# Running inverse roots of the key norms moved from SBUF into spare PSUM columns in a DeltaNet mixer

## The chip, the core and the metric

The kernel runs on one core of a Trainium2 chip. A core has five engines, each with its own instruction queue that is worked off in order: TensorE (PE in the profile; its weight loads are shown apart as PEld), VectorE (DVE), ScalarE (ACT), GpSimd (POOL) and SyncE (SP, which here only starts transfers). They share the memory SBUF; PE writes its products into PSUM, which DVE and ACT read and write too. Engines wait for each other by semaphores. The metric is the device time of one execution, in microseconds (us); durations of single instructions are also given in us unless ns is written.

## What is computed

Two layers of a diffusion trunk on 512 latent and 256 context tokens of width 1024. Layer 0 mixes tokens by a bidirectional gated DeltaNet, layer 1 by retention; each is followed by a SwiGLU block. The change touches layer 0's mixer, and in one helper every inverse root. What matters of the reference:

```python
def l2norm(t):
    tf = t.astype(jnp.float32)
    return tf * lax.rsqrt(jnp.sum(tf * tf, axis=-1, keepdims=True) + EPS)

def gdn_mixer(...):
    p = t @ w_in
    qkv = jax.nn.silu(short_conv(p[..., :GDN_QKV], conv_w))
    q = l2norm(to_heads(qkv[..., :QK_A], H_A)) * DK_A ** -0.5
    k = l2norm(to_heads(qkv[..., QK_A:2 * QK_A], H_A))
    ...
    # chunked gated delta rule over k, q, v, forward and backward; then
    # o * rsqrt(mean(o * o) + EPS) * g * silu(gate), and a projection
```

There are 8 heads of width 128. The kernel does not scale k itself: it keeps k unnormalised and puts the inverse root r of each token's squared norm, and its square, into the factors that multiply k elsewhere.

## The kernel before

All large products are exact to about fp32: each operand is split into a high and a low part and three matmuls are summed (`mm3`, L129 is the line that issues them). The heads of the DeltaNet go through a pipeline written out by hand. While PE runs the projections of head i+2 (generator `gdn_s1`, products into the PSUM tiles `psg`, of which there are 2), it also runs, interleaved in a fixed order, the triangular inverse of head i+1 (`gdn_merge`) and the output of head i (`gdn_out`). PE's instructions of this part keep the order in which the program writes them; the instructions of DVE, ACT and POOL are put in order by a scheduler ahead of time, from the program's text and an estimate of durations. At run time every engine then works off its list in order, so an instruction that waits holds back all that stand behind it on its engine.

The small tiles of this stage are `psx`: 6 PSUM tiles of 512 fp32 columns, used in rotation.

For every head, at a fixed place among the projection matmuls, `ktr` runs (heads are counted from 0):

- 6 PE transposes of the key chunks `kq` (L137), three into each of two `psx` tiles, columns 0 to 383;
- for each of these halves an ACT square into `sq` (L884), a DVE sum over it into three columns of the SBUF tile `ks` (L885), and an ACT copy of the transposed keys into `kt` (L886);
- one DVE chain on six columns: add EPS (L887), `rsqrt` (L169 and L171 give a first guess by integer arithmetic; three Newton rounds of L174, L175, L176), the norm s*r (L889), r*r (L891), and three products that give `knb`, `kbeta`, `kbd` (L894).

Around it stand these pieces, whose names the prediction uses:

- `gdn_decay`: POOL forms masks `gm` (L957, two buffers of two), PE multiplies them with `sl` into `psx`, ACT takes the exponent into `E` (L963), and POOL masks it (L964). These POOL instructions read SBUF only.
- `gdn_out` of an earlier head: ACT squares `so` (L1060), DVE sums `os` (L1061), a DVE `rsqrt` of the same 11 steps on its own tiles, then six ACT copies of `oa` scaled by that root (L1065).
- `gdn_merge`: PE products of `ysb` with `invt`, then DVE `COPY_PREDICATED` into `inva` (L1185) and a DVE transpose into `invt` (L1188), then PE products of `invt` with `U`.
- `lin`: ACT copies a finished projection out of `psg` into `pb` (L839); ACT and DVE then form the short convolution `cb` (L846, L848). `pb` also frees the `psg` tile for PE.

Of the kernel before, what the change touches and what calls it, by code (L numbers as in the profile page):

```python
# [10 lines left out]
F32 = mybir.dt.float32  # L11
# [5 lines left out]
ALU = mybir.AluOpType  # L17
AX = mybir.AxisListType
# [9 lines left out]
EPS = 1e-6  # L28
# [26 lines left out]
class Trunk:  # L55
# [80 lines left out]
    def tr(self, out, in_, ident):  # L136
        ins = self.nc.tensor.transpose(out, in_, ident)  # L137
        if self.strict:
            self.tc.keep_in_program_order(ins)
# [22 lines left out]
        self.gemm(ps, [tuple(cut(t, k) for t in w) for k in range(KT)], [tuple(t[:, a:b] for t in hk) for hk in h[st]])  # L162
        return ps

    def rsqrt(self, s, n, tag="rsq"):
        nc = self.nc
        y = self.small.tile([128, 16], F32, tag=tag + "_y", name="rsq_y")[:, :n]
        b = self.small.tile([128, 16], F32, tag=tag + "_b", name="rsq_b")[:, :n]
        nc.vector.tensor_scalar(out=y.bitcast(I32), in0=s.bitcast(I32), scalar1=1, scalar2=None,  # L169
                                op0=ALU.logical_shift_right)  # L170
        nc.vector.tensor_scalar(out=y.bitcast(I32), in0=y.bitcast(I32), scalar1=-1.0,  # L171
                                scalar2=float(0x5F3759DF), op0=ALU.mult, op1=ALU.add)
        for _ in range(3):
            nc.vector.scalar_tensor_tensor(out=b, in0=y, scalar=-0.5, in1=y, op0=ALU.mult, op1=ALU.mult)  # L174
            nc.vector.tensor_tensor(out=b, in0=b, in1=s, op=ALU.mult)  # L175
            nc.vector.scalar_tensor_tensor(out=y, in0=b, scalar=1.5, in1=y, op0=ALU.add, op1=ALU.mult)  # L176
        return y

# [682 lines left out]
    def new(self, shape, tag, dt=F32):  # L861
        return self.wk.tile(shape, dt, tag=tag, name=tag, bufs=GDN_BUFS.get(tag, 1))

    def gdn_s1(self, z, h):
        nc = self.nc
        tt, ts = nc.vector.tensor_tensor, nc.vector.tensor_scalar
        act, tr = nc.scalar.activation, self.tr
        pg = lambda: self.ps(384, "x").rearrange("p (c t) -> p c t", t=128)
        new, hd = self.new, z["hd"]
        hooks = {n: [lambda: self.gates_b()] for n in P["gates"]} if hd == 0 else {}  # L870
        yield from self.lin(1, z, h, hooks, 0)
        kb, _ = self.conv(z["pb"], 8 + hd)
        kq = z["kq"] = new([128, 6, 2, 128], "kq")
        self.silu_to(kb, kq[:, 0:2, 0, :], kq[:, 2:6, 0, :])

        def ktr():
            s = self.small.tile([128, 6], F32, tag="ks", name="ks")
            z["kt"] = kt = new([128, 6, 128], "kt")
            pss = [pg() for p in range(2)]
            for p in range(2):  # L880
                for c in range(3):
                    tr(pss[p][:, c, :], kq[:, 3 * p + c, 0, :], self.ident)
                sq = self.tmp.tile([128, 512], F32, tag="t", name="sq")[:, :384].rearrange("p (c t) -> p c t", t=128)
                act(out=sq, in_=pss[p], func=AF.Square)  # L884
                nc.vector.tensor_reduce(out=s[:, 3 * p:3 * p + 3], in_=sq, axis=AX.X, op=ALU.add)  # L885
                act(out=kt[:, 3 * p:3 * p + 3, :], in_=pss[p], func=AF.Copy)  # L886
            ts(out=s, in0=s, scalar1=EPS, scalar2=None, op0=ALU.add)  # L887
            r = self.rsqrt(s, 6, "rsk")
            tt(out=s, in0=s, in1=r, op=ALU.mult)  # L889
            z["norm"] = s  # L890
            tt(out=r, in0=r, in1=r, op=ALU.mult)  # L891
            for n in ("nb", "beta", "bd"):
                z[n] = self.small.tile([128, 2, 6], F32, tag="k" + n, name="k" + n)
                tt(out=z[n], in0=self.gd[n][:, :, :, hd], in1=r.unsqueeze(1).to_broadcast([128, 2, 6]), op=ALU.mult)  # L894

        def qsq(p):
            if p == 0:
                z["qe"] = self.small.tile([128, 6], F32, tag="qe", name="qe")
            qe, ps = z["qe"], pg()
            for c in range(3):  # L900
                tr(ps[:, c, :], z["kq"][:, 3 * p + c, 1, :], self.ident)
            sq = self.tmp.tile([128, 512], F32, tag="t", name="sq")[:, :384].rearrange("p (c t) -> p c t", t=128)
            act(out=sq, in_=ps, func=AF.Square)
            nc.vector.tensor_reduce(out=qe[:, 3 * p:3 * p + 3], in_=sq, axis=AX.X, op=ALU.add)
            if p:
                ts(out=qe, in0=qe, scalar1=EPS, scalar2=128.0 * EPS, op0=ALU.add, op1=ALU.mult)

        def vtr(p):
            vf = self.chunks(z["vb"])
            ps = pg()  # L910
            for c in range(3):
                tr(ps[:, c, :], vf(3 * p + c), self.ident)
            for c in range(3):
                act(out=z["vt"][:, 3 * p + c, :], in_=ps[:, c, :], func=AF.Copy, scale=z["norm"][:, 3 * p + c:3 * p + c + 1])

        def inv():
            with self.tc.issue_after(z["pin_v"]):
                self.gdn_inv16(z)

        gram, decay = self.gdn_gram(z), self.gdn_decay(z)  # L920
        at = lambda n, f: hooks.setdefault(n, []).append(f)
        at(H["ktr"], ktr)
        for n in range(2):
            at(H["vtr"] + n, lambda n=n: vtr(n))
            at(H["qsq"] + n, lambda n=n: qsq(n))
        for n in range(4):
            at(H["dec"] + H["ds"] * n if hd else P["d0"] + n, lambda: next(decay, None))
        for n in range(3):
            at((H["gram"] if hd else P["g0"]) + n, lambda: next(gram, None))
        if hd and H["invh"] >= 0:  # L930
            at(H["invh"], inv)
        yield from self.lin(0, z, h, hooks, 12)
        qb, _ = self.conv(z["pb"], hd)
        self.silu_to(qb, kq[:, 0:2, 1, :], kq[:, 2:6, 1, :])
        yield from self.lin(2, z, h, hooks, 24)
        z["vb"], z["pin_v"] = self.conv(z["pb"], 16 + hd)
        act(out=z["vb"], in_=z["vb"], func=AF.Silu)
        sg = z["sg"] = new([128, NT], "sg")
        z["vt"] = new([128, 6, 128], "vt")

        def evict(st, ps):
            act(out=sg[:, OFF[st]:OFF[st] + WIDTH[st]], in_=ps, func=AF.Silu)

        yield from self.units(3, z, h, evict, hooks, 36)
# [735 lines left out]
```

## Time and profile before

| | us |
|---|---|
| three runs, median (lowest to highest) | 2214.61 (2210.11 to 2215.02) |
| the profiled execution: own time | 2216.01 |
| the profiled execution: span of the trace | 2214.2 |
| PE busy in the span | 2121.5 (96%) |
| DVE busy | 1425.3 (64%) |
| ACT busy | 830.7 (38%) |
| POOL busy | 254.4 (11%) |

The granted PE clock was 0.984 of full speed on average. In the views of single instructions a row gives the start in us from the start of the span, the duration in us, engine, line, operation, the tile written and the tiles read, shapes, and a count; a bracket at its end gives the time in which the engine sat idle before it, and whose instruction ended that. The DeltaNet's heads occupy PE from about 75 to 720 us. `ktr` of the heads 0 to 7 has its transposes at 78.8, 114.1, 202.6, 275.2, 346.8, 421.9, 496.0 and 568.7 us.

### The profile page before, as it was taken

The page shows a single profiled execution, that of the slowest core. Times are in us where ns is not written, and L with a number is a line of the kernel's source. Part 1 is how long each engine was busy: PE and PEld are TensorE (multiplying, and loading weights), DVE is VectorE, ACT ScalarE, POOL GpSimd, SP SyncE. Part 2 cuts the span into 40 slices and gives each one's busy share as a digit, 9 for nine tenths or more (in the row PEclk, how much of TensorE's full clock was granted, in tenths as well). Part 3 has the DMA queues.
Part 4 walks back from the last instruction along what each step waited for, and adds up shares of the span by engine and source line. Part 5 has one row for each costly group of instructions (what it writes and reads, how often), then busy time and mean ns, then how long its engine had stood idle before and what let it go on. Part 6 is the DMA issues. An engine that isn't in the chain of part 4 may idle for free.

```text
span 2214.2 us, 34600 instructions
## 1 busy us (share of the span) xinstructions
PE 2121.5 (96%) x13998; PEld 1831.0 (83%) x13998; DVE 1425.3 (64%) x2797; ACT 830.7 (38%) x1460; POOL 254.4 (11%) x211
## 2 busy tenths in 40 slices
PE   5899999999999899999999999999999999999997
PEld 2778877788866899999899988888888888888887
DVE  5786787677755788899666774645444366433435
ACT  3656555555633543333222152222222135222212
POOL 1322112211200333334000000000000000000000
PEclk8999999999999999999999999999999999999999
DMA  6221111111175424443566541312212023322221
GB/s 241 69 56 37 45 48 42 41 43 43 33 226 175 161 111 149 143 146 129 182 216 213 168 129 36 106 46 91 77 55 84 29 77 96 115 93 88 95 72 62
DMA packets 112384, 225.09 MB, mean 102 GB/s; under 512 B 47008, under 2 KB 60320, under 8 KB 111968
## 3 DMA queue, kind: packets, MB, share of 16 engines
q1 hardware_dynamic: 100688, 192.68, 27.0%
q10 hardware_dynamic: 9360, 23.86, 3.3%
q0 software_dynamic: 2176, 6.34, 0.9%
q8 instruction: 110, 1.80, 0.3%
q14 instruction: 50, 0.41, 0.1%
HBM read 203.84 MB, written 19.01 MB: 101 GB/s over the span
## 4 chain that ended last, share of the span: by engine, by line
PE 73%; DVE 12%; DMA 5%; issue 3%; ACT 3%; POOL 0%; SPq 0%; ACTq 0%; DVEq 0%; POOLq 0%
PE psg L129 59%; PE psx L129 12%; DMA raw<-ada_t 2%; DVE wl L114 1%; DMA raw<-w 1%; DVE prod L217 1%; DVE cb L848 1%; PE psx L137 1%; DVE raw L217 1%; DMA dx<-dr 1%; DVE rsq_y L176 1%; ACT wh L113 0%; DVE rsq_b L174 0%; DVE rsq_b L175 0%; ACT vd L1021 0%
## 5 line engine op out<-in xcount | busy, mean ns | idle before, releaser
L129 PE MATMUL psg<-hh,wh 128*128 128x512 f32 (+1 forms) x1152 | 429.1, 373 | 9.9 <-ACT pb L839 6.8
L129 PE MATMUL psg<-hl,wh 128*128 128x512 f32 (+1 forms) x1152 | 423.3, 368 | 2.0 <-POOL hl L285 1.7
L129 PE MATMUL psg<-hh,wl 128*128 128x512 f32 (+1 forms) x1152 | 422.0, 367 | 0.1
L113 ACT ACTIVATE wh<-raw 128x1024 fp32r<-128x1024 f32 (+1 forms) x202 | 207.8, 1030 | 532.8 <-PE psg L129 405.8
L114 DVE TENSOR_TENSOR wl<-raw,wh 128x1024 fp32r<-128x1024 f32 (+1 forms) x202 | 254.4, 1259 | 97.8 <-ACT wh L113 94.3
L129 PEld LDWEIGHTS psg<-hh,wh 128*128 128x128 f32 x1152 | 219.9, 191 | 40.6 <-ACT pb L839 8.1
L129 PEld LDWEIGHTS psg<-hl,wh 128*128 128x128 f32 x1152 | 219.9, 191 | 32.7 <-POOL hl L285 2.1
L129 PEld LDWEIGHTS psg<-hh,wl 128*128 128x128 f32 x1152 | 220.0, 191 | 30.6 <-DVE wl L114 0.3
L129 PE MATMUL psg<-gh,w2h 128*128 128x384 f32 (+2 forms) x560 | 192.7, 348 | 6.3 <-DVE gl L114 4.4
L129 PE MATMUL psg<-gl,w2h 128*128 128x384 f32 (+2 forms) x560 | 194.2, 348 | 2.3 <-DVE gl L114 2.3
L129 PE MATMUL psg<-gh,w2l 128*128 128x384 f32 (+2 forms) x560 | 193.2, 346 | 0.0
L357 DVE SCALAR_TENSOR_TENSOR x<-psg,mod,x 128x256 f32<-128x256 f32 (+3 forms) x192 | 105.4, 570 | 114.2 <-PE psg L129 113.6
L129 PEld LDWEIGHTS psg<-gh,w2h 128*128 128x128 f32 x560 | 106.6, 191 | 13.7 <-ACT w2h L113 4.7
L129 PEld LDWEIGHTS psg<-gl,w2h 128*128 128x128 f32 x560 | 106.9, 191 | 10.3 <-DVE gl L114 4.7
L129 PEld LDWEIGHTS psg<-gh,w2l 128*128 128x128 f32 x560 | 106.6, 191 | 5.9 <-DVE w2l L114 0.4
L848 DVE SCALAR_TENSOR_TENSOR cb<-pb,k_conv_w,cb 128x770 f32<-128x770 f32 x96 | 103.7, 1081 | 7.0 <-ACT cb L846 5.6
L217 DVE CUSTOM_DVE_ANT_0 raw<-raw,crow,k_ada_b 128x1024 f32<-128x1024 f32 x54 | 79.1, 1465 | 29.3 <-DMA raw<-ada_t 28.6
L113 ACT ACTIVATE w2h<-raw 128x1024 fp32r<-128x1024 f32 x48 | 50.3, 1055 | 112.5 <-PE psg L129 81.2
L129 PE MATMUL psg<-y,wh 128*128 128x512 f32 (+1 forms) x320 | 83.3, 350 | 0.0
L129 PE MATMUL psg<-wh,hh 128*128 128x512 f32 x192 | 75.0, 391 | 0.0
L129 PE MATMUL psg<-wh,hl 128*128 128x512 f32 x192 | 74.9, 390 | 0.0
L129 PE MATMUL psg<-wl,hh 128*128 128x512 f32 x192 | 74.9, 390 | 0.0
(411 smaller groups left out, 4420.3 us busy)
## 6 DMA issues: line engine op xcount, KB each, us to landing
raw<-w SPq DMA_DIRECT2D x88, 512.0 KB, 3.6
raw<-w_ret SPq DMA_DIRECT2D x64, 512.0 KB, 3.5
raw<-ada_t SPq DMA_DIRECT2D x54, 512.0 KB, 3.5
raw<-w SPq DMA_DIRECT2D x22, 1024.0 KB, 5.4
raw<-ada_w SPq DMA_DIRECT2D x42, 512.0 KB, 5.0
raw<-w_gdn ACTq DMA_DIRECT2D x31, 512.0 KB, 3.5
graw<-gd SPq DMA_DIRECT2D x22, 384.0 KB, 4.2
gd<-g SPq DMA_DIRECT2D x40, 192.0 KB, 1.8
```

The source lines that it names most:

```text
L113: nc.scalar.activation(out=hi, in_=src, func=AF.Copy)
L114: nc.vector.tensor_tensor(out=lo, in0=src, in1=hi.bitcast(F32), op=ALU.subtract)
L129: ins = self.nc.tensor.matmul(*args, **kw)
L137: ins = self.nc.tensor.transpose(out, in_, ident)
L176: nc.vector.scalar_tensor_tensor(out=y, in0=b, scalar=1.5, in1=y, op0=ALU.add, op1=ALU.mult)
L217: nc.vector.tensor_tensor_reduce(out=out, in0=raw, in1=cb[:, v, :], scale=1.0, scalar=self.adab[:, layer, col:col + 1], op0=ALU.mult, op1= ...
L357: self.nc.vector.scalar_tensor_tensor(out=x, in0=ps, scalar=self.mod[layer][:, 24 * which + 16 + m, 1 - st:2 - st], in1=x if src is None e ...
L848: last = nc.vector.scalar_tensor_tensor(out=cb, in0=pb[:, j:j + 770], scalar=cw[:, t, j:j + 1], in1=cb, op0=ALU.mult, op1=ALU.add)
```

## The change

The two `psx` tiles of the key transposes are taken with all 512 columns. In the second of them, columns 384 to 389 (`sp`) receive the sums of squares, and columns 400 to 405 (`y`) hold the running root. The EPS step reads `sp` from PSUM and writes `ks` in SBUF; in the Newton rounds each step has one operand in PSUM and one in SBUF, for which the order of the two products is turned (y * s first, then * y) for all users of `rsqrt`. The norm gets a tile of its own, `kn`. As r*r would have two PSUM operands, r is first copied to SBUF (one more DVE instruction per head). The other users of `rsqrt` keep their SBUF tile for y.

```diff
-    def rsqrt(self, s, n, tag="rsq"):
+    def rsqrt(self, s, n, tag="rsq", y=None):
         nc = self.nc
-        y = self.small.tile([128, 16], F32, tag=tag + "_y", name="rsq_y")[:, :n]
+        if y is None:
+            y = self.small.tile([128, 16], F32, tag=tag + "_y", name="rsq_y")[:, :n]
...
         for _ in range(3):
-            nc.vector.scalar_tensor_tensor(out=b, in0=y, scalar=-0.5, in1=y, op0=ALU.mult, op1=ALU.mult)
-            nc.vector.tensor_tensor(out=b, in0=b, in1=s, op=ALU.mult)
+            nc.vector.scalar_tensor_tensor(out=b, in0=y, scalar=-0.5, in1=s, op0=ALU.mult, op1=ALU.mult)
+            nc.vector.tensor_tensor(out=b, in0=b, in1=y, op=ALU.mult)
             nc.vector.scalar_tensor_tensor(out=y, in0=b, scalar=1.5, in1=y, op0=ALU.add, op1=ALU.mult)
...
-            pss = [pg() for p in range(2)]
+            pss = [self.ps(512, "x") for p in range(2)]
+            sp, y = (pss[1][:, o:o + 6] for o in (384, 400))
+            pss = [t[:, :384].rearrange("p (c t) -> p c t", t=128) for t in pss]
             for p in range(2):
...
-                nc.vector.tensor_reduce(out=s[:, 3 * p:3 * p + 3], in_=sq, axis=AX.X, op=ALU.add)
+                nc.vector.tensor_reduce(out=sp[:, 3 * p:3 * p + 3], in_=sq, axis=AX.X, op=ALU.add)
                 act(out=kt[:, 3 * p:3 * p + 3, :], in_=pss[p], func=AF.Copy)
-            ts(out=s, in0=s, scalar1=EPS, scalar2=None, op0=ALU.add)
-            r = self.rsqrt(s, 6, "rsk")
-            tt(out=s, in0=s, in1=r, op=ALU.mult)
-            z["norm"] = s
-            tt(out=r, in0=r, in1=r, op=ALU.mult)
+            ts(out=s, in0=sp, scalar1=EPS, scalar2=None, op0=ALU.add)
+            r = self.rsqrt(s, 6, "rsk", y)
+            z["norm"] = n = self.small.tile([128, 6], F32, tag="kn", name="kn")
+            tt(out=n, in0=s, in1=r, op=ALU.mult)
+            ts(out=s, in0=r, scalar1=1.0, scalar2=None, op0=ALU.mult)
+            tt(out=r, in0=r, in1=s, op=ALU.mult)
```

The lines of the changed kernel stand 2 to 5 further down (L174 is L176 there, L885 is L889, L1188 is L1193). PE's order is the same in both programs; what changes on PE is what its instructions wait for, and on ACT and DVE the order. Three places show it.

First, PE at the key transposes of head 0. The rows name what a row waits for in brackets; `psx_760` and `psx_761` are the two tiles. Before:

```order
L137 MATMUL psx_760<-k_ident_66,kq_689 128x128 [waits PE_49,Activation_49]
L137 MATMUL psx_760<-k_ident_66,kq_689 128x128
L137 MATMUL psx_760<-k_ident_66,kq_689 128x128 [waits Activation_49]
L137 MATMUL psx_761<-k_ident_66,kq_689 128x128 x3
L129 MATMUL psx_803<-gm_799,sl0_522 128x384 [waits Pool_49]
```

Now:

```order
L137 MATMUL psx_760<-k_ident_66,kq_689 128x128 [waits PE_49,Activation_49]
L137 MATMUL psx_760<-k_ident_66,kq_689 128x128
L137 MATMUL psx_760<-k_ident_66,kq_689 128x128 [waits Activation_49]
L137 MATMUL psx_761<-k_ident_66,kq_689 128x128 [waits DVE_49]
L137 MATMUL psx_761<-k_ident_66,kq_689 128x128 x2
L129 MATMUL psx_804<-gm_800,sl0_522 128x384 [waits Pool_49]
```

The fourth transpose now waits for DVE. The instruction it waits for is the first sum of squares (L889), which writes into the tile that this transpose writes; in the program's text it stands ahead of it. It is so at all eight heads.

Second, ACT at `ktr` of head 3, from the first square to the copy of the next projection. Before (`psx_3026` and `psx_3027` are the two tiles):

```order
L884 ACTIVATE sq_3031<-psx_3026 128x384
L886 ACTIVATE kt_3025<-psx_3026 128x384
L884 ACTIVATE sq_3038<-psx_3027 128x384
L886 ACTIVATE kt_3025<-psx_3027 128x384
L963 ACT_TABLE_LOAD
L963 ACTIVATE E_2926<-psx_3068 128x384
L1065 ACTIVATE oa_2622<-oa_2622,rsq_y_2905 128x128 x6
L839 ACTIVATE pb0_542<-psg_2955 128x512
```

Now (the tiles are `psx_3029` and `psx_3030`):

```order
L888 ACTIVATE sq_3034<-psx_3029 128x384
L890 ACTIVATE kt_3028<-psx_3029 128x384
L888 ACTIVATE sq_3041<-psx_3030 128x384
L968 ACT_TABLE_LOAD
L968 ACTIVATE E_2929<-psx_3072 128x384
L1070 ACTIVATE oa_2625<-oa_2625,rsq_y_2908 128x128 x6
L890 ACTIVATE kt_3028<-psx_3030 128x384
L841 ACTIVATE pb0_542<-psg_2958 128x512
```

The second `kt` copy has moved behind the six `oa` copies, and stands right ahead of the `pb` copy. It now also waits for the second sum of squares, which writes the tile that it reads.

Third, DVE at the same head, up to the transpose into `invt`. `rsq_y_2905` is the root of `gdn_out`. Before, the two chains of roots run interleaved, and the end of the keys' chain stands ahead of `inva`:

```order
L176 SCALAR_TENSOR_TENSOR rsq_y_2905<-rsq_b_2906,rsq_y_2905 128x6
L176 SCALAR_TENSOR_TENSOR rsq_y_3043<-rsq_b_3044,rsq_y_3043 128x6
L174 SCALAR_TENSOR_TENSOR rsq_b_3044<-rsq_y_3043 128x6
L175 TENSOR_TENSOR rsq_b_3044<-rsq_b_3044,ks_3024 128x6
L176 SCALAR_TENSOR_TENSOR rsq_y_3043<-rsq_b_3044,rsq_y_3043 128x6
L889 TENSOR_TENSOR ks_3024<-ks_3024,rsq_y_3043 128x6
L891 TENSOR_TENSOR rsq_y_3043<-rsq_y_3043 128x6
L894 TENSOR_TENSOR knb_3058<-nb_747,rsq_y_3043 128x12
L894 TENSOR_TENSOR kbeta_3060<-beta_640,rsq_y_3043 128x12
L894 TENSOR_TENSOR kbd_3062<-bd_746,rsq_y_3043 128x12
L1185 COPY_PREDICATED inva_550<-k_m16_530,psx_3077 128x768
L1188 STREAM_TRANSPOSE invt_551<-inva_550 128x768
```

Now, from the last step of the root of `gdn_out` (`rsq_y_2908`) on:

```order
L178 SCALAR_TENSOR_TENSOR rsq_y_2908<-rsq_b_2909,rsq_y_2908 128x6
L891 TENSOR_SCALAR ks_3027<-psx_3030 128x6
L171 TENSOR_SCALAR psx_3030<-ks_3027 128x6
L173 TENSOR_SCALAR psx_3030<-psx_3030 128x6
L1190 COPY_PREDICATED inva_550<-k_m16_530,psx_3081 128x768
L176 SCALAR_TENSOR_TENSOR rsq_b_3046<-psx_3030,ks_3027 128x6
L1193 STREAM_TRANSPOSE invt_551<-inva_550 128x768
L177 TENSOR_TENSOR rsq_b_3046<-rsq_b_3046,psx_3030 128x6
L850 SCALAR_TENSOR_TENSOR cb_3127<-pb0_542,k_conv_w_526,cb_3127 128x770
```

The keys' chain now starts after the whole root of `gdn_out` and is spread over the work that follows. Its first step (L891) waits for the second `kt` copy on ACT, which reads the same tile, and `COPY_PREDICATED` and the transpose into `invt` stand behind it. The ACT and DVE orders at the heads 2 to 7 are as at head 3.

## The prediction

> **What bounds the kernel now.** I read the page first: the busy times, and the chain that ended last.
>
> ```profile
> PE 2121.5 (96%) x13998; PEld 1831.0 (83%) x13998; DVE 1425.3 (64%) x2797; ACT 830.7 (38%) x1460; POOL 254.4 (11%) x211
> PE 73%; DVE 12%; DMA 5%; issue 3%; ACT 3%; POOL 0%; SPq 0%; ACTq 0%; DVEq 0%; POOLq 0%
> ```
>
> PE is the bound. A saving on DVE or POOL is worth only what PE waits for it. The second view is the table by windows, for one head (us, then the busy time of PE, PEld, DVE, ACT and POOL, each with its count, the PE clock, the DMA share, GB/s); the third is the list of waits from 60 to 760 us, of which I show PE's three longest sums (total, times, longest).
>
> ```profile
> 275.00:347.00 72.00, 69.80 (x732) 57.62 (x731) 55.65 (x141) 42.63 (x94) 13.53 (x15) 1.00 0.17 45
> ```
>
> ```profile
> PE psg L129 <- ACT pb L839: 6.8, 6, 1.3
> PE psx L129 <- POOL gm L957: 4.3, 7, 2.3
> PE psx L129 <- DVE invt L1188: 3.2, 6, 0.6
> ```
>
> In a head PE idles 2.2 us of 72. The waits for `pb` and for `invt` are the places where something in the neighbourhood of `ktr` is late for PE. The timeline of PE at head 3 shows both:
>
> ```profile
> 275.19 0.82 PE L137 MATMUL psx<-k_ident,kq 128*128 128x128 f32 x6
> 275.76 0.59 PE L129 MATMUL psx<-gm,sl 128*128 128x384 f32 x2
> ...
> 284.57 0.50 PE L129 MATMUL psg<-hh,wh 128*128 128x512 f32 x1 [1.11 <-ACT pb L839]
> 285.61 0.56 PE L129 MATMUL psx<-invt,U 64*64 64x64 f32 x12 [0.54 <-DVE invt L1188]
> ```
>
> So there is 1.65 us per head to win, and nothing more. Both waits hang on DVE: `pb` stands on ACT behind the six `oa`, which wait for the root of `gdn_out`; `invt` stands on DVE behind both chains of roots.
>
> **What the change is to relieve.** POOL's timeline of the same stretch, and four rows of DVE:
>
> ```profile
> 276.27 0.83 POOL L957 TENSOR_TENSOR gm<-ut,ghi 128x384 fp32r<-128x384 f32 x1 [1.39 <-PE psx L129]
> 277.06 0.83 POOL L957 TENSOR_TENSOR gm<-ut,glo 128x384 fp32r<-128x384 f32 x1
> 279.24 1.03 POOL L964 TENSOR_TENSOR E<-E,ut 128x384 f32<-128x384 f32 x1 [1.35 <-ACT E L963]
> 280.24 0.83 POOL L957 TENSOR_TENSOR gm<-ut,ghi 128x384 fp32r<-128x384 f32 x1
> 281.03 0.83 POOL L957 TENSOR_TENSOR gm<-ut,glo 128x384 fp32r<-128x384 f32 x1
> ```
>
> ```profile
> 281.12 0.76 DVE L175 TENSOR_TENSOR rsq_b<-rsq_b,os 128x6 f32<-128x6 f32 x1
> ...
> 282.39 0.17 DVE L175 TENSOR_TENSOR rsq_b<-rsq_b,ks 128x6 f32<-128x6 f32 x1
> 282.59 0.17 DVE L176 SCALAR_TENSOR_TENSOR rsq_y<-rsq_b,rsq_y 128x6 f32<-128x6 f32 x1
> ```
>
> A step on six columns takes 0.17 us, and chained steps follow each other by 0.20. While POOL runs, the same step takes 0.76: it ends with POOL's instruction (281.12 + 0.76 = 281.88; POOL's 281.03 + 0.83 = 281.86). Under POOL, DVE makes about one such step per POOL instruction. A DVE step with an operand in PSUM escapes that:
>
> ```profile
> 268.25 0.89 POOL L957 TENSOR_TENSOR gm<-ut,ghi 128x384 fp32r<-128x384 f32 x1 [17.36 <-PE psx L129]
> ```
>
> ```profile
> 268.36 0.29 DVE L1044 TENSOR_TENSOR oa<-oa,psx 128x128 f32<-128x128 f32 x1
> ```
>
> It started and ended inside POOL's instruction. So the keys' steps, now with one PSUM operand, should no longer be held. The root of `gdn_out`, however, stays in SBUF and is held as before. The price of a keys' step with a PSUM operand lies between the 0.17 of an SBUF step and the 0.29 of this row with 128 columns; I take 0.17 to 0.20, as six columns are nearer to the former. The other end costs at most 0.12 x 3 steps ahead of `invt` (L891, L171, L173) x 6 heads, 2.2 us in all.
>
> The row above has 128 columns and one PSUM operand. [...]
>
> **What the change adds, at head 3** (heads 2 to 7 have this order). (a) A wait of PE. The fourth transpose now waits for the first sum of squares. Two ACT rows and the first sum:
>
> ```profile
> 275.72 0.49 ACT L884 ACTIVATE sq<-psx 128x384 f32<-128x384 f32 x1 [0.51 <-PE psx L137]
> 276.11 0.48 ACT L886 ACTIVATE kt<-psx 128x384 f32<-128x384 f32 x1
> ```
>
> ```profile
> 276.24 0.55 DVE L885 TENSOR_REDUCE ks<-sq 128x3 f32<-128x384 f32 x1 [0.57 <-ACT sq L884]
> ```
>
> The sum ends at 276.79, so the fourth transpose starts at 276.84; it stood at about 275.52 (half way through the six). PE is 1.32 late from here, and queued behind it stand all projections and L129's `gm,sl`, at 277.08 in place of 275.76.
>
> [...]
>
> (b) The root of `gdn_out` (11 steps, with the second sum after the seventh) now runs first. POOL's first `gm` starts 0.51 behind PE's `gm,sl` (276.27 against 275.76), so now at 277.59, and the pair ends at 279.2. From 276.8 on, DVE does five steps till 277.75, and one under each `gm`: seven by 279.2. The second sum takes 0.55, to 279.8. ACT's rows give the next POOL instruction:
>
> ```profile
> 277.38 1.28 ACT L963 ACT_TABLE_LOAD   x1
> 278.67 0.49 ACT L963 ACTIVATE E<-psx 128x384 f32<-128x384 f32 x1
> 282.18 1.87 ACT L1065 ACTIVATE oa<-oa,rsq_y 128x128 f32<-128x128 f32 x6 [3.01 <-DVE rsq_y L176]
> 283.95 0.57 ACT L839 ACTIVATE pb<-psg 128x512 f32<-128x512 f32 x1
> ```
>
> The second square follows the last transpose and ends at about 277.9; table load and `E` take it to 279.6; POOL's mask of `E` runs 279.6 to 280.6, its next pair to 282.2. So one step is held by `E` and two by the pair, and the eleventh ends at 282.5. `oa` starts at 282.6, 0.4 later than in the row.
>
> (c) On ACT the second `kt` copy now stands behind `oa`. The copy starts 1.77 after `oa` (283.95 - 282.18, the place that `pb` had), at 284.37, and ends at 284.85; `pb` follows 0.39 behind its start (276.11 - 275.72), at 284.76. PE's projection followed `pb` by 0.62 (284.57 - 283.95): now 285.38, 0.8 late. PE itself would be there at 284.57 - 1.11 + 1.32 = 284.78, so the stall (a) is covered by the wait for `pb`, which shrinks to 0.6. This covers (a); without it PE's 1.32 would stand in full.
>
> (d) On DVE the keys' chain begins with L891, which waits for that `kt` copy, so at 284.88; behind it in the queue stand L171, L173, then `inva` and `invt`, whose rows before are
>
> ```profile
> 283.44 1.01 DVE L1185 COPY_PREDICATED inva<-k_m,psx 128x768 f32<-128x768 int32 x1
> 284.49 0.98 DVE L1188 STREAM_TRANSPOSE invt<-inva 128x768 f32<-128x768 f32 x1
> ```
>
> Two chained steps at 0.20 and one that is independent at 0.1 bring `inva` to 285.4, 2.0 late; one more step of the chain stands ahead of `invt`, 286.55. PE's products followed the start of `invt` by 1.12 (285.61 - 284.49): 287.67, **2.1 us late**. PE waits for nothing else there, and the 1.32 and 0.8 are contained in the 2.1. What comes behind (`cb`, `wl`, the rest of the chain, `U`) is late by less, and PE has more than 2 us of other work ahead of it; I cost it at nothing. If that cover is gone, it costs up to 1.7 per head, the delay of `U`. Six heads: 6 x 2.1 = **12.6**.
>
> All of it hangs on one time, the end of the root of `gdn_out`: a later end by x moves `invt` by x. The loss is that end less 280.5 or so; ending there, `invt` comes as before.
>
> **Heads 0 and 1** have no root of `gdn_out` beside them, so only (a) counts, against a shorter chain. Rows of PE and DVE:
>
> ```profile
> 78.77 1.18 PE L137 MATMUL psx<-k_ident,kq 128*128 128x128 f32 x6 [0.51 <-ACT kq L858]
> ```
>
> ```profile
> 82.02 1.00 DVE L885 TENSOR_REDUCE ks<-sq 128x3 f32<-128x384 f32 x2
> ...
> 85.23 0.93 DVE L174 SCALAR_TENSOR_TENSOR rsq_b<-rsq_y 128x6 f32<-128x6 f32 x1
> ...
> 114.69 4.96 DVE L848 SCALAR_TENSOR_TENSOR cb<-pb,k_conv_w,cb 128x770 f32<-128x770 f32 x3
> 119.57 1.00 DVE L885 TENSOR_REDUCE ks<-sq 128x3 f32<-128x384 f32 x2
> ```
>
> ```profile
> 98.14 0.50 PE L129 MATMUL psg<-hh,wh 128*128 128x512 f32 x1 [1.27 <-ACT pb L839]
> ...
> 114.08 0.81 PE L137 MATMUL psx<-k_ident,kq 128*128 128x128 f32 x6
> ...
> 115.52 0.44 PE L129 MATMUL psx<-gm,sl 128*128 128x384 f32 x1 [0.44 <-POOL gm L957]
> ...
> 120.39 0.44 PE L129 MATMUL psx<-gm,sl 128*128 128x384 f32 x1 [2.34 <-POOL gm L957]
> 121.18 0.44 PE L129 MATMUL psx<-gm,sl 128*128 128x384 f32 x1 [0.35 <-POOL gm L957]
> ```
>
> In both, DVE is busy with other work when the squares are ready, and PE now waits for that: at head 0 from about 79.2 to 82.1 to 82.6, of which its later wait of 1.27 gives back a part, net +1.4 to +1.8. At head 1 DVE's queue ahead of the sum is as long as before and starts up to 1.4 later, so the sum ends between 120.1 and 121.5; with 120.8, the work of PE from the fourth transpose (114.41) to 121.18, less its three waits there (0.44 + 2.34 + 0.35 = 3.13), 3.64 us, ends at 124.4 in place of 121.18. The two heads together: **+3.2** (1.7 to 4.7, by that spread and the gain of the steps that took 0.93).
>
> **Sum:** 2216.01 (the profiled execution) + 12.6 + 3.2 = 2231.8. The median of the runs lies 1.4 lower, so I predict 2230.
>
> **Rivals.** (A) *The root clears POOL, and the time is not longer.* If the order of arrival lets the last four steps of `gdn_out` run before POOL's mask of `E` (the second sum earlier, or `E` later by some 0.8), it ends at about 279.5. Then `pb` and `invt` are early, the waits of 1.11 and 0.54 vanish, and only (a) is left: 1.32 - 1.65 = -0.33 per head. With heads 0 and 1 between -4 (the stall all paid by waits that vanish) and +3.2 this gives 2214.6 - 2.0 - 4 to + 3.2: 2209 to 2216; with (a) at 1.6 it is near 2218. It decides at 280.5. For it speaks that 0.8 us separates the cases; against it that POOL's instructions follow PE's stall just as DVE's do. 0.20. (B) *Slower still:* the chain's end (`kbd`, `U`) or the later release of the `psx` tile, now held until `kbd`, is late for PE too. By the 1.7 of `U` that is up to 6 x 1.7 = 10 more, 2240. Against it: the next user of that tile on PE comes about 3 us after `kbd`. 0.10. (C) *The steps are held in PSUM as well*, so nothing is relieved: heads 2 to 7 remain as forecast, as their keys' chain runs behind POOL anyway; head 0 and 1 lose their gain, some +3. That is 2233. Against it stands the row at 268.36. 0.05. (D) *Faster:* the root ends early, and the shorter chains of head 0 and 1 let the convolutions and `wl` come early for PE: (A)'s low end with the rest of PE's idle 2.2 us per head cut by a half, 2214.6 - 6 x 1.1 - 2: 2206. 0.05.
>
> **Chances.** The forecast, 2224 to 2236, has 0.60; A 0.20, B 0.10, C 0.05, D 0.05. What a measurement of this kernel can tell from no change is about 0.3%, 6.6 us: 2208 to 2221.2. Slower: forecast, B and C, 0.75, and A's tail, 0.01: 0.76. Within: A, 0.18. Faster: D and A's low end, 0.06. The range takes in A's upper part and B: 2213 to 2242.
>
> **What would show it.** (a): at all heads PE's fourth transpose waits some 1.3 us for DVE L889. (b): the root of `gdn_out` ends near 282.5 on the scale of head 3, with steps of 0.8 in it, and the keys' steps all near 0.2. (c): ACT's second `kt` copy idles behind no DVE sum but follows `oa`; PE's wait for `pb` halves. (d): PE's wait for `invt` grows from 0.54 to about 2. If PE's wait for `invt` is gone, A was right; if PE waits for `U` or a `psx` tile, B; if keys' steps of 0.8 remain, C. Wrong would be the forecast if the root's steps are not held.

## The result, and the profile after

The changed kernel takes 2230.66 us (median of 4 runs, 2229.54 to 2231.44), the kernel before 2212.36 us (4 runs, 2209.96 to 2215.02): a ratio of 1.0079, 95% interval 1.0064 to 1.0093. The forecast was 2230. The total was right, in part by luck: as the rows show, one large term came out less than half as big as I wrote, and waits that I had put at nothing made up for it.

The page of the changed kernel, busy times and the chain that ended last:

```profile
PE 2119.1 (95%) x13998; PEld 1831.0 (82%) x13998; DVE 1414.2 (63%) x2805; ACT 832.8 (37%) x1460; POOL 255.9 (11%) x211
PE 73%; DVE 12%; DMA 5%; ACT 4%; issue 3%; POOL 0%; SPq 0%; DVEq 0%; ACTq 0%; POOLq 0%
```

PE's instructions are the same. DVE is busy 11 us less, though it has 8 instructions more: its steps are held less by POOL: of the DeltaNet's steps on 6 or 12 columns, 18 take longer than 0.35 us, and 42 did before; each of these ends within 0.06 us of a POOL instruction. So the change does what it says, and the time rises all the same. The waits of PE from 60 to 760 us say why:

```profile
PE psx L137 <- DVE psx L889: 12.7, 8, 3.1
PE psx L129 <- DVE rsq_b L177: 7.3, 6, 1.2
PE psx L129 <- DVE S L1039: 5.3, 8, 2.0
PE psx L129 <- DVE R L1014: 3.9, 1, 3.9
```

The wait for `pb` (6.8 us before) is gone from the list, that for `invt` (3.2 us before) is the second row: the profile names L177, which stands right behind the transpose into `invt`. Three rows are new. `S` is the running state of a head's output stage, `R` a tile that is formed from it and that PE multiplies next. The first new row is the stall at the fourth transpose, at all eight heads. Head 3 on PE, and what it waited for:

```profile
280.40 0.55 PE L137 MATMUL psx<-k_ident,kq 128*128 128x128 f32 x3 [1.18 <-DVE psx L889]
280.71 0.59 PE L129 MATMUL psx<-gm,sl 128*128 128x384 f32 x2
...
288.26 0.39 PE L129 MATMUL psg<-hh,wh 128*128 128x512 f32 x1
289.86 0.56 PE L129 MATMUL psx<-invt,U 64*64 64x64 f32 x12 [1.21 <-DVE rsq_b L177]
```

Here the first three transposes start at 278.74 (275.19 before). The products of `invt` start 11.12 us behind them, and did 10.42 before: 0.70 us at this head, where I had 2.1. (It is the same at the heads 2 to 6; at head 7, where PE did not wait for `pb` before, they start at 11.11 in place of 9.26, 1.85 us later.) Why it is less stands in DVE's and POOL's rows of the same stretch:

```profile
281.26 0.80 DVE L176 SCALAR_TENSOR_TENSOR rsq_b<-rsq_y,os 128x6 f32<-128x6 f32 x1
282.10 0.76 DVE L177 TENSOR_TENSOR rsq_b<-rsq_b,rsq_y 128x6 f32<-128x6 f32 x1
282.78 0.55 DVE L889 TENSOR_REDUCE psx<-sq 128x3 f32<-128x384 f32 x1
283.24 0.15 DVE L178 SCALAR_TENSOR_TENSOR rsq_y<-rsq_b,rsq_y 128x6 f32<-128x6 f32 x1
283.43 0.96 DVE L176 SCALAR_TENSOR_TENSOR rsq_b<-rsq_y,os 128x6 f32<-128x6 f32 x1
284.43 0.17 DVE L177 TENSOR_TENSOR rsq_b<-rsq_b,rsq_y 128x6 f32<-128x6 f32 x1
284.63 0.17 DVE L178 SCALAR_TENSOR_TENSOR rsq_y<-rsq_b,rsq_y 128x6 f32<-128x6 f32 x1
287.16 0.17 DVE L891 TENSOR_SCALAR ks<-psx 128x6 f32<-128x6 f32 x1 [2.37 <-ACT kt L890]
```

```profile
283.37 1.00 POOL L969 TENSOR_TENSOR E<-E,ut 128x384 f32<-128x384 f32 x1 [0.53 <-ACT E L968]
284.82 0.84 POOL L962 TENSOR_TENSOR gm<-ut,ghi 128x384 fp32r<-128x384 f32 x1 [0.45 <-PE psx L129]
```

POOL's next `gm` waits 0.45 us for PE's `gm,sl`, which the stall made late; in that gap DVE does the last two steps of `gdn_out`'s root at 0.17 us each. I had put the `gm` right behind the mask of `E`, and the two steps under it. The root ends at 284.80, 6.06 us behind the first transpose, not 7.3. On the scale of the kernel before that is 281.25, and by the prediction's own rule (the loss at `invt` is that end less 280.5 or so) it makes 0.75 us, against the 0.70 measured. The last row shows the rest of step (d) as forecast: DVE idles 2.37 us for the second `kt` copy, which stands behind `oa` on ACT.

**Where the 18 us lie.** I cut the DeltaNet from head 0's first key transpose to the last head's first products of `S` (78.77 to 682.58 before), and took from windows of 1 us how long PE was idle, and what the granted clock cost (PE busy time by one less the clock, summed). Each line is one profiled execution beside the median of its runs; ratios are against the runs of before on the same chip.

| kernel | median, us | ratio (95%) | PE idle, us | clock, us |
|---|---|---|---|---|
| before | 2212.36 | | 22.4 | 11.9 |
| changed | 2230.66 | 1.0079 (1.0064 to 1.0093) | 37.4 | 11.0 |
| changed, again (e8) | 2226.40 | 1.0060 (1.0046 to 1.0074) | 35.0 | 5.9 |
| e4 arithmetic alone | 2214.71 | 1.0009 (0.9993 to 1.0025) | 25.4 | 1.7 |
| e1 root in PSUM | 2213.39 | 1.0003 (0.9989 to 1.0017) | 24.8 | 6.5 |
| e2 sums in PSUM | 2229.36 | 1.0066 (1.0043 to 1.0089) | 37.1 | 3.3 |
| e3 both, used in turn | 2212.61 | 0.9996 (0.9984 to 1.0009) | 21.5 | 5.1 |
| e5 stall | 2229.96 | 1.0070 (1.0056 to 1.0083) | 37.4 | 15.5 |
| e10 stall, `invt` first | 2223.92 | 1.0041 (1.0027 to 1.0056) | 38.3 | 4.6 |
| e6 late `kt` | 2229.86 | 1.0077 (1.0063 to 1.0091) | 34.9 | 17.0 |
| e7 both roots in PSUM | 2244.71 | 1.0140 (1.0126 to 1.0154) | 42.9 | 16.8 |
| e9 the same, `invt` first | 2225.44 | 1.0042 (1.0027 to 1.0057) | 31.5 | 1.7 |
| e11 heads 0 and 1 | 2218.49 | 1.0029 (1.0017 to 1.0041) | 26.5 | 11.1 |
| e12 heads 2 to 7 | 2225.38 | 1.0059 (1.0046 to 1.0073) | 34.7 | 5.1 |

PE's idle time belongs to the program: 21 to 27 us in the kernels within 0.3% of before, 31 to 43 in the others, 37.4 and 35.0 in two profiles of the changed kernel. The clock's share goes from 1.7 to 17 and differs by 5 between these two. A profiled execution can lie well off the median of its kernel: e2's lies 9.0 and e9's 7.0 us below it, e6's and e10's 5.2 above, so the last two columns don't add up to differences of the medians.

### The profile page after: what moved, and what is told of

Same layout as the page of the kernel before. It is cut to its first block, busy times and chain, and to the rows that moved or that the text cites. A ratio compares the mean times of both kernels' runs of the same rounds, so it can differ in the third digit from the quotient of the medians.

```text
span 2229.3 us, 34631 instructions
## 1 busy us (share of the span) xinstructions
PE 2119.1 (95%) x13998; PEld 1831.0 (82%) x13998; DVE 1414.2 (63%) x2805; ACT 832.8 (37%) x1460; POOL 255.9 (11%) x211
## 4 chain that ended last, share of the span: by engine, by line
PE 73%; DVE 12%; DMA 5%; ACT 4%; issue 3%; POOL 0%; SPq 0%; DVEq 0%; ACTq 0%; POOLq 0%
PE psg L129 60%; PE psx L129 12%; DVE wl L114 2%; DMA raw<-ada_t 1%; DVE prod L219 1%; DMA raw<-w 1%; PE psx L137 1%; DVE cb L850 1%; DMA raw<-w_ret 1%; DVE rsq_b L176 1%; DVE raw L219 1%; DMA dx<-dr 1%; ACT oa L1070 1%; ACT wh L113 1%; DMA dr<-x 0%
```

## The experiments

My theory after the trace: the loss is made of waits that come from the sharing of one PSUM tile (PE's stall; the second `kt` copy that waits for a sum and lands behind `oa`) and not of the price of any step. The rivals are in the expectations.

**e4, the arithmetic alone.** Sums and root in SBUF, turned Newton products, `kn` and the copy of r kept (changed kernel with `s` for `sp`, no `y`).

```diff
-                nc.vector.tensor_reduce(out=sp[:, 3 * p:3 * p + 3], ...)
+                nc.vector.tensor_reduce(out=s[:, 3 * p:3 * p + 3], ...)
-            ts(out=s, in0=sp, scalar1=EPS, ...)
-            r = self.rsqrt(s, 6, "rsk", y)
+            ts(out=s, in0=s, scalar1=EPS, ...)
+            r = self.rsqrt(s, 6, "rsk")
```

> Only the arithmetic of the change: products of the Newton rounds in the turned order, the tile kn, and the copy of r; sums and root in SBUF. My theory: no effect that can be told, 2208 to 2217. Rival A (the additional copy and the moved order of DVE are a part of the loss): 2219 or more.

1.0009: no effect that can be told. Rival A falls.

**e1, the root alone in PSUM**, and **e2, the sums alone in PSUM**: the first two of the three changed lines of e4, or the last.

> The sums of squares go to SBUF as before the change; the running root stays in the PSUM columns. My theory: the loss comes from waits that the shared tile makes (PE's fourth transpose for the first sum, the second kt copy behind the scaled outputs) and not from the price of a PSUM step, so this kernel loses all of it: no PE wait for DVE at the fourth key transpose, keys' steps of 0.2 us free of POOL, time 2204 to 2215. Rival P (steps with a PSUM operand are dear or still held by POOL): it stays slow, 2222 to 2232, with keys' steps of 0.3 us or more.

> The sums of squares stay in the PSUM columns, the running root goes back to SBUF. My theory: this keeps PE's wait of 1.2 us at the six later heads and about 3 us at the first two, and the kt copy behind the scaled outputs, so it keeps most of the loss: 2220 to 2230, the lower part if the wait of 3.9 us for R in the last head, which the order of this kernel doesn't have, belongs to the order. Rival P (the root in PSUM is the cost): 2208 to 2216.

e1 is as fast as before (1.0003), e2 as slow as the whole change (1.0066). So the PSUM operand of the Newton steps costs nothing that can be told, and the two small sums in the shared tile cost all of it. The waits of e2 hold the stall unchanged:

```profile
PE psx L137 <- DVE psx L889: 12.7, 8, 3.1
PE psx L129 <- DVE rsq_y L178: 8.9, 6, 1.5
PE psx L129 <- ACT kq L860: 4.5, 5, 0.9
```

The second row is again the wait for `invt`. The third stands at five heads; the kernel before has no row like it above 0.5 us.

**e3, both in PSUM, but used in turn.** All transposes, squares and copies are written ahead of the sums.

```diff
             for p in range(2):
                 for c in range(3):
                     tr(pss[p][:, c, :], kq[:, 3 * p + c, 0, :], self.ident)
+            sqs = []
+            for p in range(2):
...
-                nc.vector.tensor_reduce(out=sp[...], in_=sq, ...)
                 act(out=kt[:, 3 * p:3 * p + 3, :], in_=pss[p], func=AF.Copy)
+                sqs.append(sq)
+            for p, sq in enumerate(sqs):
+                nc.vector.tensor_reduce(out=sp[...], in_=sq, ...)
```

> Sums and root both in the PSUM columns as in the change, but all six transposes, both squares and both kt copies are written ahead of the two sums. My theory: the cost was the order in which the shared tile was used, so without the two waits it is as fast as before or faster: 2204 to 2216, no PE wait at the fourth transpose, kt copies early on ACT. Rival B (any shared use of the bank costs, since its release for PE is late or DVE and ACT shut each other out): 2222 or more, with PE waiting for psx slots.

As fast as before (0.9996): shared columns cost nothing in this order, and rival B falls. But nothing is won either, since the waits for `invt` (the profile names L898, which stands right behind it) and `pb` are still there:

```profile
PE psx L129 <- DVE kn L898: 4.6, 6, 0.8
PE psg L129 <- ACT pb L841: 4.4, 5, 0.9
```

Before they were 3.2 and 6.8 us: `pb` waits for the root of `gdn_out`, which stays in SBUF (in the changed kernel's rows above POOL still holds it, at 0.76 to 0.96 us a step); what the keys' chain gains ends up in front of `invt`, interleaved with that root.

**e5, the stall without the late copy** (each `kt` copy written ahead of its half's sum), and **e6, the late copy without the stall** (all transposes written first, the rest as in the change).

```diff
-                nc.vector.tensor_reduce(out=sp[...], in_=sq, ...)
                 act(out=kt[:, 3 * p:3 * p + 3, :], in_=pss[p], func=AF.Copy)
+                nc.vector.tensor_reduce(out=sp[...], in_=sq, ...)
```

> As the changed kernel, but each kt copy is written ahead of the sum of its half, so the second copy doesn't wait for the second sum: PE's wait at the fourth transpose stays, the late kt copy goes. My theory: the stall of 1.2 us at the six later heads (partly covered by the wait for pb that was there before) and 2.6 and 3.1 us at the first two remain: 2217 to 2225, with PE waiting 11 to 13 us in all for the first sum, and a wait for invt no longer than before. Rival K (the late kt copy is the whole loss and the stall is covered): 2210 to 2216. Rival S (the stall is the whole loss): 2226 or more.

> As the changed kernel, but all six transposes are written first: PE no longer waits for the first sum, while ACT's second square and second kt copy still wait for DVE's sums and the kt copy stands behind the scaled outputs. My theory: the late invt (1.2 us or more per head) and the late U stay, and the order of the last head with a weight's low part between two R steps is in this kernel too: 2218 to 2228. Rival K: 2226 or more. Rival S: 2210 to 2217.

Each alone is as slow as both (1.0070, 1.0077), against my expectation for either: e5 ended where rival S had it, e6 where rival K had it, and both cannot hold. In e5 another order on DVE is a part of it: a convolution step stands between the copy into `inva` and the transpose into `invt`, and PE waits 2.1 us for `invt` at each of six heads.

```profile
290.94 1.04 DVE L1190 COPY_PREDICATED inva<-k_m,psx 128x768 f32<-128x768 int32 x1
291.87 1.00 DVE L850 SCALAR_TENSOR_TENSOR cb<-pb,k_conv_w,cb 128x770 f32<-128x770 f32 x1
292.79 0.97 DVE L1193 STREAM_TRANSPOSE invt<-inva 128x768 f32<-128x768 f32 x1
```

**e10** is e5 with priority on DVE for these two (`with self.tc.high_priority():` around L1190 and L1193), which puts them together.

> As the kernel with PE's stall alone (kt copies written ahead of the sums), with the same priority for inva and invt. My theory: what made that kernel as slow as the whole change was a convolution step between inva and invt (PE waited 2.1 us for invt in each of six heads); without it, the stall alone costs 5 to 6 us at the first two heads and little in the other six, where it stands in for the waits for pb and invt: 2217 to 2223. If the stall costs its full 12.6 us wherever it is put, 2225 to 2229.

1.0041, at 2223.92 just above my range: the stall, with the DVE order of this kernel, costs 9 us (6 to 12 by the interval). In its profile PE waits 12.6 us for the first sum, and 7.0 for `invt` in six heads, while `pb` is no longer waited for. Rival S falls with that. Rival K, that the late copy is the whole loss, falls too, as there is a loss without the late copy. That the two halves do not add because both delay the same `invt` is my reading, not shown: in e6 PE's waits are others (S 7.7 us, `invt` 7.5, `pb` 5.6, R 3.3), in e10 there are 4.1 us for `kq` at five heads, so e5, e6 and e10 don't split the sum cleanly. What the priority alone does to the kernel before was not run.

**e7, both roots in PSUM**: e1 and the root of `gdn_out` in a `psx` tile of its own, the last step writing SBUF; **e9** is e7 with the priority of e10.

```diff
-        r = self.rsqrt(s, 6, "rso")
+        r = self.small.tile([128, 16], F32, tag="rso_r", name="rso_r")[:, :6]
+        self.rsqrt(s, 6, "rso", self.ps(512, "x")[:, 400:406], r)
```

> The kernel with the sums in SBUF and the keys' root in PSUM, with the root of gdn_out also in a psx tile of its own (its last step writes SBUF). My theory: POOL then holds neither chain, the scaled outputs leave ACT earlier, and the waits for pb and invt of 1.65 us per head go: 2198 to 2208. Rival N (the additional psx tile in the rotation makes PE wait for slots): 2212 or more, with PE waiting for DVE or ACT at psx tiles.

> As the kernel with both roots in PSUM, but the masked copy into inva and the transpose into invt have priority on DVE, so no convolution step stands between them any more. My theory: its loss of 30 us was the wait for invt (20.9 us in six heads, behind two convolution steps), so this takes 18 to 22 us off: 2220 to 2228, and what is left above before are PE's 18 waits for gm of POOL (10.9 us, against 4.3 us before). If all of the loss was the moved order of DVE, it ends near 2203 to 2210. Rival N (the additional tile in the rotation): 2238 or more.

e7 is the slowest kernel of all (1.0140): convolution steps now stand between `inva` and `invt` (20.9 us of waiting in six heads). With the priority 19 us of it go (1.0042); what is left are 10.9 us for `gm` in 18 waits and 7.8 for `invt`, ahead of which a low part `wl` now stands. Rival N falls: no wait for a `psx` slot is among the longer ones. Neither beats the kernel before, and I found no version that does. e9's rows do show the relief itself; DVE and POOL at one moment:

```profile
276.45 0.55 DVE L891 TENSOR_SCALAR ks<-ks 128x6 f32<-128x6 f32 x1
277.14 0.17 DVE L171 TENSOR_SCALAR psx<-ks 128x6 int32<-128x6 int32 x1
277.34 0.17 DVE L173 TENSOR_SCALAR psx<-psx 128x6 int32<-128x6 int32 x1
```

```profile
276.14 0.84 POOL L962 TENSOR_TENSOR gm<-ut,glo 128x384 fp32r<-128x384 f32 x1
276.93 1.03 POOL L969 TENSOR_TENSOR E<-E,ut 128x384 f32<-128x384 f32 x1
```

The step on SBUF alone ends with POOL's instruction; the two that touch PSUM run inside the next one at 0.17 us. In all of e9, none of the 200 DVE steps on six columns that touch PSUM takes longer than 0.18 us; in the kernel before, where all 216 such steps are on SBUF alone, 42 take longer than 0.35.

**e8, the changed kernel again.**

> The changed kernel once more, for a second profile beside the others. If the clock's drops fall at other places than in its first profile while the waits stay, the waits belong to the program and the drops' places to the execution: waits of PE for the first sum 12 to 13 us in all, the wait for R 3.5 to 4.5 us in the last head, time 2226 to 2233.

1.0060, a median of 2226.40 and a profile of 2224.91 (2231.05 the first): the waits are the same (12.7, 7.4), S and R somewhat less (3.7, 3.1; I had expected 3.5 to 4.5 for R), and the clock fell elsewhere.

**e11 and e12, the change at some heads only** (`hd < 2` or `hd >= 2` chooses `sp` and `y`, else SBUF).

> The change at heads 0 and 1 only; the other six keep sums and root in SBUF. The prediction's term for these two heads was +3.2 (1.7 to 4.7), so some 2217. My theory after the traces: PE waits 2.6 and 3.1 us for the first sum, and for gm behind it, and its clock drops after these waits, so +5 to +9: 2219 to 2223. If these heads cost nothing: 2212 to 2215.

> The change at heads 2 to 7 only. The prediction's term was 6 x 2.1 = +12.6, all as a wait for invt of about 2 us per head: some 2226. My theory after the traces: the wait for invt takes 1.2 us per head, which with the stall and the vanished wait for pb is +0.75 a head (4.5), and the rest are waits for S (2 to 5) and for R in the last head (3 to 4): +9 to +13, 2223 to 2227. If the loss was all at the first two heads: 2212 to 2216.

Heads 0 and 1: +5.3 us (2218.49 against 2213.16; by the interval of the ratio 3.8 to 9.1). Heads 2 to 7: +12.2 (10.2 to 16.2). Together 17.5; the whole change cost 18.3. Both lie in the ranges that I had expected after the traces, as differences.

## Why the prediction came out right, step by step

- **The bound** held: from profile to profile the time rose by 15.0 us, and PE's idle time in the DeltaNet by 15.0. **What could be won**, 1.65 us per head, no kernel won: e3 takes the stall away and keeps the relief, and the time stays.
- **The price of a PSUM step** (0.17 to 0.20 taken): 0.17 in the rows, and none of the changed kernel's 120 steps on six columns that touch PSUM takes longer than 0.20. Right.
- **(a), the stall of 1.32 us:** 1.18 at each of the six heads. Right.
- **(b), the end of `gdn_out`'s root** at 7.3 us behind the first transpose: 6.06. This is the step that I mis-timed, and (d) hangs on it. I moved POOL's first pair with PE's stall, but not its second, which PE's stall moves too.
- **(c):** the wait for `pb` did not halve but vanished, as `oa` came 1.3 us earlier than forecast (6.15 us behind the first transpose, not 7.41).
- **(d):** 0.70 us net at five heads and 1.85 at the last, 5.3 in six, not 12.6. The mechanism (the copy behind `oa`, DVE idle for it, `inva` and `invt` behind) is there row by row.
- **"What comes behind ... I cost it at nothing"** is the step that failed, and it made up for (d); that the two errors nearly cancel, 12.2 us measured against 12.6, is luck. I had priced it (up to 1.7 per head, in rival B) and given it 0.10. `U` comes 1.65 us later (19.2 us behind the first transpose; 17.5 in e4), and on ACT the copies of `dg`, which start the DMA round trip for the next inverse, now stand behind a weight's `wh`. The changed kernel, then e4, at head 3:

```profile
306.40 1.06 ACT L113 ACTIVATE wh<-raw 128x1024 fp32r<-128x1024 f32 x1 [2.90 <-PE psg L129]
307.37 1.47 ACT L1088 ACTIVATE dg<-U 32x192 f32<-32x192 f32 x4
```

```profile
301.63 1.48 ACT L1088 ACTIVATE dg<-U 32x192 f32<-32x192 f32 x4 [1.32 <-DVE U L987]
304.06 1.06 ACT L113 ACTIVATE wh<-raw 128x1024 fp32r<-128x1024 f32 x1
```

  DVE's first step on the returned data, in the changed kernel:

```profile
316.66 0.16 DVE L1120 TENSOR_TENSOR p<-x,v 96x2 f32<-96x2 f32 x1 [1.50 <-DMA v<-dr]
```

  That is 37.9 us behind the first transpose (34.6 in e4, without idle time), and behind it in DVE's list stands the copy of `S` that PE needs: PE waits 1.2 us here, and 2.0 at head 5. How long the transfers take differs by 2 us from head to head (`v` lands 2.1 to 4.2 us after its issue), and the step's start from one execution to the next: in e8 it is at 36.4, and PE waits 0.3 us at this head. Why, I did not test.
- **The last head** was in no term. DVE's order puts the low part of a weight between two steps of `R`, and that weight's transfer is late (6.1 us from issue to landing; ACT's `wh` idles 4.35 us for it):

```profile
628.98 0.35 DVE L1014 SCALAR_TENSOR_TENSOR R<-psx,negc,vt 128x128 f32<-128x128 f32 x1 [0.74 <-PE psx L129]
632.94 0.69 DVE L114 TENSOR_TENSOR wl<-raw,wh 128x512 fp32r<-128x512 f32 x1 [3.60 <-ACT wh L113]
633.54 0.34 DVE L1014 SCALAR_TENSOR_TENSOR R<-psx,negc,vt 128x128 f32<-128x128 f32 x1
```

```profile
633.95 0.79 PE L129 MATMUL psx<-R,W 128*128 128x128 f32 x2 [3.88 <-DVE R L1014]
```

  PE waits 3.88 us. e6, e8 and e12 have the same order and wait 3.3, 3.1 and 3.4. e2 has neither this wait nor the late `S`, and is as slow: its wait for `invt` is longer (8.9 us), and there are the 4.5 us for `kq`. So `S` and `R` are not a fixed amount on top of the rest. In the first profile PE's idle time behind head 1 grows by 12.2 us: 5.3 for (d), 5.1 for `S`, 3.9 for `R`, less some 2 for shorter waits elsewhere. That split holds for this one execution.
- **Heads 0 and 1:** +3.2 (1.7 to 4.7) forecast, +5.3 measured (3.8 to 9.1). At head 0 PE waits 2.58 us for the first sum (2.9 to 3.4 forecast), and then, which I had not in the sum, 1.48 and 1.32 us for `gm`, whose POOL instructions follow PE: the same omission as in (b), with the other sign. So it comes later to head 1 and waits 3.07 us there, not the 5 or so that 120.8 would have made; they stand in place of three waits for `gm`, 3.13 us, which are gone. The clock had no term in the prediction: up to head 2 it costs 3.3 to 6.1 us in the profiles with the change at these heads (the first, e2, e8, e11) and 1.7 without it (before, e4, e12), while PE idles 9.0 to 9.2 us against 6.3 to 8.1. So by these profiles some half of the 5.3 is the clock.
- **The rivals:** A fell (the root does end earlier, but the wait for the late `kt` copy stays on the path), C fell by e9's rows, D had nothing for it. B was half right: `U` is late and costs PE time, but PE waits for `S` behind it, and no wait for a `psx` slot held until `kbd` is among the longer ones.

## What to carry to other kernels

Free columns of a PSUM tile that other engines still write and read were not free here: in this program a step put there between two uses of the tile makes the later use wait for it (1.18 us at six heads, 2.6 and 3.1 at the others). These are waits that the program carries; whether the chip would need them, no run tested. Here it was enough to finish every use of one kind before the next began (e3). Before an engine's steps are relieved, look up which step PE in fact waits for; the keys' chain was not it. And where a scheduler sets the order, read the whole order against the old one, to the last head: the convolution steps that moved ahead of `invt` cost e7 19 us and e5 6 us, by the medians with and without the priority.

## What the runs showed of the hardware that was not expected

PE's granted clock fell to one half after rather short waits. Windows of the kernel before, at a place where PE had waited 1.13 and 0.54 us within 2.2 us (the columns as in the prediction):

```profile
354.00:356.00 2.00, 1.07 (x9) 0.87 (x8) 1.85 (x8) 2.00 (x7) 0.00 (x0) 1.00 0.00 0
356.00:358.00 2.00, 1.26 (x13) 0.94 (x13) 1.68 (x3) 2.00 (x4) 1.01 (x1) 0.81 0.00 0
358.00:360.00 2.00, 2.00 (x17) 1.37 (x15) 2.00 (x3) 0.81 (x3) 0.00 (x0) 0.50 0.00 0
360.00:362.00 2.00, 2.00 (x24) 1.35 (x25) 1.93 (x3) 0.24 (x1) 0.00 (x0) 0.50 0.49 129
362.00:364.00 2.00, 2.00 (x12) 1.59 (x9) 0.60 (x1) 1.60 (x2) 0.00 (x0) 0.50 0.33 133
364.00:366.00 2.00, 2.00 (x13) 1.67 (x13) 1.19 (x2) 1.11 (x3) 0.46 (x1) 0.98 0.03 8
```

The missing clock is (0.19 + 0.50 x 3 + 0.02) x 2 us = 3.4 us, a stretch of 6.8 us at half speed. Other drops cost 1.7, half as much (in the kernel before, the two windows from 507 to 511 us have 0.61 and 0.54). The pair of waits for `pb` and `invt` stands at 25 places in the profiles of before, e1, e3, e4 and e11 (heads 2 to 6), and a drop follows at 10 of them: 4, 1, 2, 0 and 3. In e6 the pair is 1.1 and 1.25 us, and a drop follows at all five heads. In the changed order the same idle time is cut in two, 1.18 and 1.21 us, 8 us apart, and no drop follows either at any of 24 places (both profiles, e2 and e12). So the change also took something away; it gave it back behind the waits for S and R and at the first two heads. Why a drop comes at some of equal places and not at others, no run shows. Whether the drops make most of the spread of equal runs (2208 to 2219 us for all but one run of before) was not tested.
